# Score products of the recurrent phase in one chain of turns per half, one gate block and the later pins moved

## The chip, the cores and the metric

The kernel runs on one core of a Trainium2 chip. The metric is the device time of one execution in microseconds (us), the median of several runs. The core's engines work beside each other, each through a queue of its own in a fixed order: TensorE (PE, matrix products into PSUM), VectorE (DVE), ScalarE (ACT), GpSimd (POOL), and the queues that issue transfers.

## The reference

One layer of an encoder on `x` of 2048 positions by 1024 features, in float32. It mixes chunked band attention with a recurrent branch (time mixing by a delta rule), and ends with a squared-relu feed-forward. The change touches the recurrent branch:

```python
def step(state, inp):
    r_t, w_t, k_t, v_t, aa_t, bb_t = inp
    sa = jnp.einsum('bhij,bhj->bhi', state, aa_t)
    state = (state * w_t[:, :, None, :] + sa[..., None] * bb_t[:, :, None, :]
             + v_t[..., None] * k_t[:, :, None, :])
    y = jnp.einsum('bhij,bhj->bhi', state, r_t)
    return state, y
...
h = rms_norm(x, pre_mix_g[l])
proj = h @ w_in[l]
...
y_a = chunk_band_attention(q.reshape(shp), k.reshape(shp), v.reshape(shp), rel_bias[l])
y_b = rwkv7_time_mix(p_rwkv, shift_mu[l], w0[l], w2[l], a0[l], a2[l], g2[l],
                     k_k[l], k_a[l], r_k[l], ln_x_w[l], ln_x_b[l])
merged = gate_a * (y_a @ proj_a[l]) + gate_b * (y_b @ proj_b[l])
x = x + rms_norm(merged @ w_out[l], post_mix_g[l])
```

The recurrence runs over all positions for 8 heads of 64. The output of each head is normalised, gets a bonus term and is multiplied by a gate.

## The kernel before

**Groups and phases.** The positions are worked on in 4 groups of 512. Each group passes a recurrent phase (`phase_rwkv`), an attention phase and a merge; after all groups comes the feed-forward. The recurrent phase begins near 25 us of the span in group 0 and repeats every 466 to 496 us.

**The dense matmuls.** The projection by `w_in` is the bulk of TensorE's work there. A block of 128 columns (`dense`) is 24 matmuls of 128x512 in single-pass form: each operand is split into a high and a low part, and 8 each of high by high (`hh,whi`), low by high (`hl,whi`) and high by low (`hh,wlo`) are summed. ACT makes `whi` (L80) and DVE `wlo` (L82). The list `dl` holds the dense matmuls of the phase in their order. A gate block is a `dense` whose result goes through a tanh to memory; nothing in the phase waits for it, so gate blocks fill TensorE while others work.

**The pins.** `place(mm, n)` puts the matmul `mm` behind `dl[n]` in TensorE's queue (`queue_behind`, an order without a semaphore). The tables `BLOCKS`, `TURNED`, `FIFTH`, `BONUS` and `SCORES` hold such numbers. What isn't pinned, and every other engine's order, comes from the program's order and the scheduler that builds the queues.

**The recurrent branch.** The 8 heads are 4 pairs, p = 0 to 3; 512 positions are 8 chunks of 64. Pairs 0 and 1 go through the branch together, then pairs 2 and 3:

1. `rwkv_pre` makes a pair's operands on DVE and ACT, with squared sums (`ps_ss`, L486), bonus (`ps_bonus`, L553) and transposes (`ps_bk`, L564) by TensorE.
2. The **score products** `ps_A` (L584) multiply the operands of 4 chunks at a time (a half), 4 products by the upper 64 rows into one bank of PSUM and 4 by the lower 64 into another. The pool `pa` has two banks, for all that carries the tag "a", the low-rank products `ps_z` and `ps_a` (L427, L428) too. DVE empties each bank by four operations into `NA` (L595, two), `AR` (L601) and `BR` (L602). In the program the two banks take turns product by product; only the first product of pair 0 is pinned.
3. `rwkv_inverse` inverts triangular blocks on DVE: a transpose `N` (L610), 31 steps of `T` and `X` (L620, L626), a transpose `X1` (L629). It runs once for pairs 0 and 1 and once for pairs 2 and 3.
4. `rwkv_blocks` and `rwkv_trans` (`ps_t` L651 and L659, `ps_at` L679, `ps_w`, `ps_ug`, `ps_tq`, `ps_s` L722) make each chunk's transition from it. The first `ps_t` needs `X1`.
5. The chunks follow in order (`rwkv_chunk`): `ps_st` (L737) and `ps_y` (L741) on TensorE, then the state `ST` or `st` on DVE (L742), which the next chunk needs.
6. `rwkv_post` normalises: a square on ACT, a sum `var` on DVE (L755), `var` and a root `grs` on POOL (L756, L758), the product `yn` on DVE (L760), 8 transposes `ps_yt` on TensorE (L769), written out by ACT to `yf` (L774), and the gate `ps_g`.

The steps of pairs 2 and 3 up to their score products run between the steps 4 and 5 of pairs 0 and 1; the steps 6 of pairs 0 and 1 run while the second inverse works.

Of the kernel before, what the change touches and what calls it, by code (L numbers as in the profile page):

```python
# [32 lines left out]

GATES = (0, 0, 1, 0, 0, 0, 0, 1)
STEPS = (1, 2, 1, 1, 1, 1, 1, 1, 1, 1, 1, 0, 0, 2, 1)
BLOCKS = ((412, 424), (631, 644))
TURNED = 438
FIFTH = 494
BONUS = {(0, 1): 138, (1, 0): 258}
SCORES = 150  # L40
DEC = math.exp(-0.5)

ATT0 = 0
# [4 lines left out]
def advance(steps, n=None):  # L48

    while n is None or n > 0:  # L50
        if next(steps, steps) is steps:
            return
        n = n and n - 1


class Block:
# [387 lines left out]
    def rwkv_pre(self, g, p, rp, NA, between=lambda: None):  # L444
        nc = self.nc
# [7 lines left out]
        ps = self.lora(0, p)  # L453
# [5 lines left out]
        ps = self.lora(1, p)  # L459
# [92 lines left out]
        for i, x in enumerate((rh, rl)):  # L552
            mm = nc.tensor.matmul(psb, self.bones, x, start=i == 0, stop=i == 1)  # L553
# [22 lines left out]
        for h in range(2):  # L576
            cs = slice(h * 4, h * 4 + 4)

            both = [self.pa.tile([P, 4, P], F32, tag="a", name="ps_A") for _ in range(2)]
            for j in range(4):  # L580
                c = h * 4 + j
                for par, psA in enumerate(both):
                    rw = slice(par * C, par * C + C)
                    mm = nc.tensor.matmul(  # L584
                        psA[:, j].rearrange("p (s t) -> p s t", t=C),
                        BK[rw, c].rearrange("p s t -> p (s t)"),
                        AR[rw, c, par : 3 : 2 - par], start=True, stop=True,
                    )
                    if p == c == par == 0:
                        self.place(mm, SCORES)  # L590
            for par, psA in enumerate(both):
                ow = slice(C - par * C, P - par * C)
                for lo, w in ((0, C), (32, 32)):
                    hw = slice(par * C + lo, par * C + lo + 32)
                    nc.vector.tensor_tensor(  # L595
                        NA[hw, q, cs, 0:w],
                        psA[hw, :, lo : lo + w],
                        n2[hw, cs, par, None].to_broadcast((32, 4, w)),
                        ALU.mult,
                    )  # L600
                nc.vector.tensor_tensor(AR[ow, cs, par], psA[ow, :, 0:C], mS[ow], ALU.mult)  # L601
                nc.vector.tensor_tensor(BR[:, cs, par, 1], psA[:, :, C:P], mN[:, par, cs], ALU.mult)  # L602
# [38 lines left out]
    def rwkv_blocks(self, NA, Rs, b):  # L641
# [14 lines left out]
        for q in range(2):  # L656
            for c in range(NC):
                for lo, hi in parts:
                    mm = nc.tensor.matmul(ps[lo, q, c], Z[hi, q, c], XT[hi, q, c, 32:64], start=True, stop=True)  # L659
                    second.append(mm)  # L660
        for mm, n in zip((first[0], second[0]), BLOCKS[b]):
            self.place(mm, n)
# [5 lines left out]
    def rwkv_trans(self, p, R):  # L668
# [7 lines left out]
        for h, cs in enumerate(halves):  # L676
            ps = self.pa.tile([P, 4, P], F32, tag="a", name="ps_at")
            for j in range(4):
                mm = nc.tensor.transpose(ps[:, j], AR[:, h * 4 + j, 0:2].rearrange("p s t -> p (s t)"), self.ident)  # L679
                if p == 0 and h == 1 and j == 0:  # L680
                    self.place(mm, TURNED)
            for par in range(2):
# [47 lines left out]
    def rwkv_chunk(self, p, c, R):  # L730
# [5 lines left out]
        for r in rows:  # L736
            mm = nc.tensor.matmul(ps[r], TQ[r, c, 0], S[r], start=True, stop=True)  # L737
            if p == 0 and c == 4 and r.start == 0:
                self.place(mm, FIFTH)
        for r in rows:  # L740
# [6 lines left out]
    def rwkv_post(self, p, R):  # L747
        nc = self.nc
        pc = slice(p * P, (p + 1) * P)
        col = slice(p, p + 1)  # L750
        Y = R["Y"]
        yq = self.tmp("yq").rearrange("p (c t) -> p c t", t=C)
        nc.scalar.activation(yq, Y, AF.Square)
        var = self.sp.tile([P, NC], F32, tag="var", bufs=2, name="var")
        nc.vector.tensor_reduce(var, yq, AX.X, ALU.add)  # L755
        nc.gpsimd.tensor_scalar(var, var, 1.0 / C, GN_EPS, ALU.mult, ALU.add)  # L756
        rs = self.sp.tile([P, NC], F32, tag="grs", bufs=2, name="grs")
        nc.gpsimd.tensor_tensor(rs, var, self.nhalf, ALU.pow)  # L758
        yn = self.tmp("yn").rearrange("p (c t) -> p c t", t=C)
        nc.vector.tensor_tensor(yn, Y, rs[:, :, None].to_broadcast((P, NC, C)), ALU.mult)  # L760
        bv = self.tmp("bv")
        nc.sync.dma_start(bv, self.bvd[p])
        yield
        yf = self.tmp("yf")
        yf3 = yf.rearrange("p (c t) -> p c t", t=C)
        for h in range(2):
            ps = self.pr.tile([C, 4, P], F32, tag="wus", name="ps_yt")
            for j in range(4):
                nc.tensor.transpose(ps[:, j], yn[:, h * 4 + j], self.ident)  # L769
            cs = slice(h * 4, h * 4 + 4)  # L770
            nc.scalar.activation(
                yf3[0:C, cs], ps[:, :, 0:C], AF.Identity, scale=self.gw[0:C, col], bias=self.gb[0:C, col]
            )
            nc.scalar.activation(  # L774
                yf3[C:P, cs], ps[:, :, C:P], AF.Identity, scale=self.gwo[:, col], bias=self.gbo[:, col]
            )
        self.tc.keep_in_program_order(nc.vector.tensor_tensor(yf, yf, bv, ALU.add))
        ps = self.py.tile([P, G], F32, tag="y", name="ps_g")
        self.mm3(ps, [(*(x[:, pc] for x in self.g2), *self.lg)])
        nc.vector.tensor_tensor(yf, yf, ps, ALU.mult)  # L780
        nc.gpsimd.dma_start(self.yd[p], yf)
# [8 lines left out]
    def phase_rwkv(self, g, quads):  # L790
        tc = self.tc
        with ExitStack() as ctx:
# [18 lines left out]
            def gate(n=1):  # L811
                for i in range(n):
                    i = next(gates, None)
                    if i is not None:
                        self.gate(i)
# [12 lines left out]
            def rec_of(NA, Rs, b):  # L828
                self.rwkv_blocks(NA, Rs, b)
                yield  # L830
                for q in range(2):
                    yield from self.rwkv_trans(2 * b + q, Rs[q])
                    yield
                yield from self.recurrence(b, Rs)
# [13 lines left out]
            advance(inv, 6)  # L848
            self.lora_g(g)
            advance(inv)  # L850
            gate()
            rec = rec_of(NA, Rs, 0)
            NA = pairs()
            between = places(STEPS, lambda n: advance(rec, n))
# [15 lines left out]
            for i in range(3):  # L870
# [5 lines left out]
                elif i == 1:  # L876
                    b, c = (rp.tile([P, n, G], F32, tag=t, name="cmb") for t, n in (("AR", 3), ("SV", 2)))
# [763 lines left out]
```

## Time and profile before

| | us |
|---|---|
| median of 3 runs (lowest to highest) | 3209.29 (3207.58 to 3210.35) |
| the profiled execution | 3213.15 |
| its span, first to last instruction | 3211.4 |
| TensorE busy | 3155.3 (98%) |
| VectorE busy | 2236.4 (70%) |
| ScalarE busy | 1577.5 (49%) |
| GpSimd busy | 614.0 (19%) |
| mean granted TensorE clock | 0.998 |

A row of a timeline has the start and the length in us, engine, line, operation, output and inputs, shapes, and a count; in brackets the idle time before it and what ended it. Rows with a count run several instructions together, and pipelined matmuls overlap, so the time that a run of them takes is read from the start of one row to the start of the next. One score product appears as two records of 64 rows, so x16 are the 8 products of a half. A row of waits has the waiting operation, the operation waited for, and us in all, times, and the longest.

### The profile page before, as it was taken

How to read it: one execution, taken by the hardware profiler on the slowest of the kernel's cores; microseconds unless marked ns; L12 is line 12 of the kernel's file. 1: busy time of each engine (PE TensorE's matmuls, PEld its weight loads, DVE VectorE, ACT ScalarE, POOL GpSimd, SP SyncE). 2: the span in 40 equal slices, each digit the busy share in tenths (PEclk: the TensorE clock that was granted, in tenths of full speed). 3: DMA queues.
4: the chain of work that ended last, by engine and by line, in shares of the span. 5: the costliest groups of instructions: out<-in, count | busy, mean ns of one | idle time of the engine just before them, and what ended most of it. 6: DMA issues, size and time to landing. Idle time of an engine off the chain costs nothing. (4 is left out here: it accounts for less than half of the span.)

```text
span 3211.4 us, 49808 instructions
## 1 busy us (share of the span) xinstructions
PE 3155.3 (98%) x18800; PEld 2574.0 (80%) x18800; DVE 2236.4 (70%) x3668; ACT 1577.5 (49%) x2511; POOL 614.0 (19%) x1119
## 2 busy tenths in 40 slices
PE   8999999999999999999999999999999999999998
PEld 6877788777888878888877888888888878888887
DVE  6785667776767786766876775887656668765464
ACT  5435645445745444745534755544543454444343
POOL 3222012132112222112222110122211112210000
PEclk9999999999999999999999999999999999999999
DMA  6245474257574247575336557554887876447565
GB/s 190 85 136 183 134 260 128 60 171 240 178 258 127 78 141 243 178 233 164 96 112 223 168 191 267 191 174 160 290 277 246 282 229 213 164 161 238 195 220 174
DMA packets 436069, 598.82 MB, mean 186 GB/s; under 512 B 25570, under 2 KB 296044, under 8 KB 435828
## 3 DMA queue, kind: packets, MB, share of 16 engines
q1 hardware_dynamic: 377716, 415.24, 41.1%
q0 software_dynamic: 48896, 163.61, 13.8%
q10 hardware_dynamic: 9216, 16.78, 1.4%
q8 instruction: 148, 2.42, 0.3%
q14 instruction: 93, 0.76, 0.1%
HBM read 431.67 MB, written 167.01 MB: 186 GB/s over the span
## 5 line engine op out<-in xcount | busy, mean ns | idle before, releaser
L1465 PE MATMUL ps_dn<-fop 128*128 128x512 f32 x2688 | 610.8, 389 | 0.0
L1465 PEld LDWEIGHTS ps_dn<-fop 128*128 128x128 f32 x2688 | 504.2, 188 | 104.7 <-DVE fop L82 0.3
L80 ACT CAST whi<-wraw 128x1024 fp32r<-128x1024 f32 x232 | 243.4, 1049 | 317.8 <-PE psd L91 235.0
L82 DVE TENSOR_TENSOR wlo<-wraw,whi 128x1024 fp32r<-128x1024 f32 x230 | 280.7, 1220 | 150.0 <-ACT whi L80 96.6
L91 PE MATMUL psd<-hh,whi 128*128 128x512 f32 x1328 | 362.5, 400 | 1.1 <-ACT k L400 1.1
L91 PE MATMUL psd<-hh,wlo 128*128 128x512 f32 x1328 | 356.9, 397 | 0.0
L91 PE MATMUL psd<-hl,whi 128*128 128x512 f32 x1328 | 353.9, 396 | 0.0
L91 PEld LDWEIGHTS psd<-hl,whi 128*128 128x128 f32 x1328 | 244.2, 188 | 48.4
L91 PEld LDWEIGHTS psd<-hh,wlo 128*128 128x128 f32 x1328 | 243.0, 188 | 47.6
L91 PEld LDWEIGHTS psd<-hh,whi 128*128 128x128 f32 x1328 | 240.8, 189 | 49.8 <-ACT k L400 1.6
L82 DVE TENSOR_TENSOR fop<-xraw,fop 128x1024 fp32r<-128x1024 f32 x112 | 137.0, 1223 | 176.5 <-ACT fop L80 176.0
L80 ACT CAST fop<-xraw 128x1024 fp32r<-128x1024 f32 x112 | 117.7, 1051 | 251.2 <-PE ps_dn L1465 188.8
L1335 POOL DMA_DIRECT2D xd<-X x192 | 103.7, 540 | 379.6 <-ACT X L1332 313.3
L82 DVE TENSOR_TENSOR fop<-wdraw,fop 128x1024 fp32r<-128x1024 f32 x112 | 136.6, 1220 | 19.1 <-ACT fop L80 18.6
L80 ACT CAST fop<-wdraw 128x1024 fp32r<-128x1024 f32 x112 | 117.8, 1052 | 36.6 <-DMA wdraw<-in_w_down_dram 20.5
L991 DVE CUSTOM_DVE_ANT_0 sc<-bias,ps_s 128x640 f32<-128x640 f32 (+4 forms) x128 | 93.8, 733 | 48.2 <-PE ps_s L985 24.9
L998 ACT ACTIVATE sc<-sc,mn 128x640 f32<-128x640 f32 (+4 forms) x128 | 97.7, 764 | 27.8 <-DVE mn L991 26.4
L1009 DVE TENSOR_TENSOR PTl<-ps_pt,PTh 128x640 fp32r<-128x640 f32 (+4 forms) x128 | 94.4, 738 | 23.8 <-ACT PTh L1008 22.3
L80 ACT CAST s12h<-s 128x1024 fp32r<-128x1024 f32 x32 | 33.7, 1054 | 156.3 <-PE ps_u L91 155.1
L91 PE MATMUL ps_p<-yh,whi 128*128 128x512 f32 x256 | 101.7, 402 | 2.7 <-ACT yh L80 2.1
L1174 PE MATMUL ps_o<-whi,mh 128*128 128x512 f32 x256 | 100.6, 393 | 2.8 <-DVE o L1185 2.8
L1008 ACT CAST PTh<-ps_pt 128x640 fp32r<-128x640 f32 (+4 forms) x128 | 79.9, 624 | 47.6 <-PE ps_pt L1004 45.8
(374 smaller groups left out, 6854.0 us busy)
## 6 DMA issues: line engine op xcount, KB each, us to landing
wraw<-in_w_in_dram SPq DMA_DIRECT2D x168, 512.0 KB, 4.0
xraw<-xd SPq DMA_DIRECT2D x112, 512.0 KB, 4.5
xd<-X POOLq DMA_DIRECT2D x192, 256.0 KB, 5.1
wraw<-in_w_up_dram SPq DMA_DIRECT2D x80, 512.0 KB, 5.1
wdraw<-wd SPq DMA_DIRECT2D x64, 512.0 KB, 4.8
wdraw<-in_w_down_dram SPq DMA_DIRECT2D x48, 512.0 KB, 5.2
gd<-gate ACTq DMA_DIRECT2D x64, 256.0 KB, 2.4
wd<-cmb POOLq DMA_DIRECT2D x64, 256.0 KB, 3.8
```

The costliest lines, as they stand in the source:

```text
L80: high = self.high = self.nc.scalar.copy(hi, src)
L82: self.low = lower.tensor_tensor(lo, src, hi.bitcast(F32), ALU.subtract).ins
L91: mm.append(nc.tensor.matmul(ps, l, r, start=n == 0, stop=n == last).ins)
L991: least = nc.vector.tensor_tensor_reduce(sc[:, 0:n], bias[:, s0:640], pss[:, c0 : c0 + n], 1.0, 3.0e38, ALU.add, ALU.min, mn,)
L998: nc.scalar.activation(sc[:, 0:n], sc[:, 0:n], AF.Exp, scale=-1.0, bias=mn, accum_out=sm[:, col : col + 1])
L1008: nc.scalar.copy(hv, pst[:, 0:nk])
L1009: nc.vector.tensor_tensor(lv, pst[:, 0:nk], hv.bitcast(F32), ALU.subtract)
L1174: nc.tensor.matmul(ps[t], l[:, k, ts], r[:, k % 2], start=k == 0 and j == 0, stop=k == KB - 1 and j == 2)
L1335: nc.gpsimd.dma_start(self.xd[q][i // 2][:, i % 2], src)
L1465: nc.tensor.matmul(ps, o[:, l, k, sl], o[:, r, k], start=start and n == 0, stop=stop and n == end)
```

## The change

The products of a half form one chain in TensorE's queue, in turns between the two banks. The first product of every half of every pair is pinned by a table `SCORES[p][h]`, where before only that of pair 0 was, and its first number, 150, stays. The transposes `ps_yt` of pair 1 are pinned by a table `TURNS`. A gate block more stands ahead of the first `rwkv_blocks`, so that all gate blocks behind it come one earlier. The pins of `BLOCKS`, `TURNED` and `FIFTH` follow: the first by 24, the length of a block; the second pair of `BLOCKS` by 9.

```diff
--- before.py
+++ after.py
@@ -33,11 +33,12 @@
 
 GATES = (0, 0, 1, 0, 0, 0, 0, 1)
 STEPS = (1, 2, 1, 1, 1, 1, 1, 1, 1, 1, 1, 0, 0, 2, 1)
-BLOCKS = ((412, 424), (631, 644))
-TURNED = 438
-FIFTH = 494
+BLOCKS = ((436, 448), (640, 653))
+TURNED = 462
+FIFTH = 518
 BONUS = {(0, 1): 138, (1, 0): 258}
-SCORES = 150
+SCORES = ((150, 162), (266, 278), (476, 479), (528, 538))
+TURNS = {1: (612, 616)}
 DEC = math.exp(-0.5)
 
 ATT0 = 0
@@ -577,6 +578,7 @@
             cs = slice(h * 4, h * 4 + 4)
 
             both = [self.pa.tile([P, 4, P], F32, tag="a", name="ps_A") for _ in range(2)]
+            last = None
             for j in range(4):
                 c = h * 4 + j
                 for par, psA in enumerate(both):
@@ -586,8 +588,11 @@
                         BK[rw, c].rearrange("p s t -> p (s t)"),
                         AR[rw, c, par : 3 : 2 - par], start=True, stop=True,
                     )
-                    if p == c == par == 0:
-                        self.place(mm, SCORES)
+                    if last is None:
+                        self.place(mm, SCORES[p][h])
+                    else:
+                        self.queue_behind(mm.ins, last)
+                    last = mm.ins
             for par, psA in enumerate(both):
                 ow = slice(C - par * C, P - par * C)
                 for lo, w in ((0, C), (32, 32)):
@@ -766,7 +771,9 @@
         for h in range(2):
             ps = self.pr.tile([C, 4, P], F32, tag="wus", name="ps_yt")
             for j in range(4):
-                nc.tensor.transpose(ps[:, j], yn[:, h * 4 + j], self.ident)
+                mm = nc.tensor.transpose(ps[:, j], yn[:, h * 4 + j], self.ident)
+                if j == 0 and p in TURNS:
+                    self.place(mm, TURNS[p][h])
             cs = slice(h * 4, h * 4 + 4)
             nc.scalar.activation(
                 yf3[0:C, cs], ps[:, :, 0:C], AF.Identity, scale=self.gw[0:C, col], bias=self.gb[0:C, col]
@@ -848,7 +855,7 @@
             advance(inv, 6)
             self.lora_g(g)
             advance(inv)
-            gate()
+            gate(2)
             rec = rec_of(NA, Rs, 0)
             NA = pairs()
             between = places(STEPS, lambda n: advance(rec, n))
```

Lines below the new tables shift by one, and by two to five behind the new statements (L584 is L586, L737 is L742, L769 is L774). Three places in the queues show what moves.

TensorE from the end of pair 1's transition (`ps_s`) to the first chunks of pairs 0 and 1, between which pair 2's score products and the low-rank products of pair 3 stand. Before:

```order
L722 MATMUL ps_s_1742<-SV,BR 64x64 x16
L584 MATMUL ps_A<-AR,BK 128x128 x8
L91 MATMUL psd<-hh,wlo 128x512 x4
L584 MATMUL ps_A<-AR,BK 128x128 x4
L91 MATMUL psd<-hh,wlo 128x512 x2
L584 MATMUL ps_A<-AR,BK 128x128 x4
L737 MATMUL ps_st<-st_101,TQ 64x64 x2
L741 MATMUL ps_y<-st_101,TQ 64x64 x2
L737 MATMUL ps_st<-st_102,TQ 64x64 x2
L741 MATMUL ps_y<-st_102,TQ 64x64
L427 MATMUL ps_z<-lora,whw 128x512
L428 MATMUL ps_z<-lora,wlw 128x512
```

and of the change:

```order
L727 MATMUL ps_s_1776<-SV,BR 64x64 x16
L92 MATMUL psd<-hh,wlo 128x512 x3
L586 MATMUL ps_A<-AR,BK 128x128 x8
L92 MATMUL psd<-hh,wlo 128x512 x3
L742 MATMUL ps_st<-st_101,TQ 64x64 x2
L746 MATMUL ps_y<-st_101,TQ 64x64 x2
L742 MATMUL ps_st<-st_102,TQ 64x64 x2
L746 MATMUL ps_y<-st_102,TQ 64x64 x2
L586 MATMUL ps_A<-AR,BK 128x128 x8
L742 MATMUL ps_st<-ST,TQ 64x64 x2
L746 MATMUL ps_y<-ST,TQ 64x64 x2
L742 MATMUL ps_st<-ST,TQ 64x64 x2
```

The first half has moved behind 3 dense matmuls and the second behind one chunk of both pairs, each in one row of 8; the second, in two rows of 4 before with 2 dense between, has 3 dense and a chunk ahead of it instead of 4 dense; `ps_z` and `ps_a`, the next behind the second piece's end, now follow two whole chunks.

VectorE behind the first half of pair 3's score products, where the last states of pairs 0 and 1 (`st`), the sums and products of `rwkv_post` and the start of the second inverse (`N`) meet. Before:

```order
L601 TENSOR_TENSOR AR<-ps_A,mS 64x4x64
L602 TENSOR_TENSOR BR<-ps_A,mN 128x4x64
L742 SCALAR_TENSOR_TENSOR st_101<-ps_st,gC,S_1577 128x64
L742 SCALAR_TENSOR_TENSOR st_102<-ps_st,gC,S_1741 128x64
L755 TENSOR_REDUCE var<-yq 128x8
L610 STREAM_TRANSPOSE N<-NA 128x1024
L760 TENSOR_TENSOR yn<-ps_y,grs 128x512
L755 TENSOR_REDUCE var<-yq 128x8
L620 TENSOR_TENSOR T<-N,X 128x31
L82 TENSOR_TENSOR wlo<-wraw,whi 128x1024
L760 TENSOR_TENSOR yn<-ps_y,grs 128x512
```

and of the change:

```order
L760 TENSOR_REDUCE var<-yq 128x8
L765 TENSOR_TENSOR yn<-ps_y,grs 128x512
L600 TENSOR_TENSOR NA<-ps_A,n_2027 32x256
L600 TENSOR_TENSOR NA<-ps_A,n_2027 32x4x32
L606 TENSOR_TENSOR AR<-ps_A,mS 64x4x64
L607 TENSOR_TENSOR BR<-ps_A,mN 128x4x64
L600 TENSOR_TENSOR NA<-ps_A,n_2027 32x256
L600 TENSOR_TENSOR NA<-ps_A,n_2027 32x4x32
L606 TENSOR_TENSOR AR<-ps_A,mS 64x4x64
L607 TENSOR_TENSOR BR<-ps_A,mN 128x4x64
L760 TENSOR_REDUCE var<-yq 128x8
L615 STREAM_TRANSPOSE N<-NA 128x1024
```

The first `yn` stood behind the evacuations of the second half and behind `N`; it now stands ahead of these evacuations, directly behind its `var`, and `N` stands behind both.

TensorE from pair 1's output transposes to the first `ps_t` of the second inverse. Before:

```order
L91 MATMUL psd<-hh,whi 128x512
L769 MATMUL ps_yt<-ident,yn 64x128 x4
L91 MATMUL psd<-hh,whi 128x512 x2
L769 MATMUL ps_yt<-ident,yn 64x128 x4
L91 MATMUL psd<-hh,whi 128x512 x5
L91 MATMUL psd<-hl,whi 128x512 x8
L91 MATMUL psd<-hh,wlo 128x512 x8
L91 MATMUL psd<-hh,whi 128x512 x8
L91 MATMUL psd<-hl,whi 128x512 x8
L91 MATMUL psd<-hh,wlo 128x512 x8
L91 MATMUL psd<-hh,whi 128x512 x8
L651 MATMUL ps_t_2512<-X_2414,NA 32x32 x32
```

and of the change:

```order
L92 MATMUL ps_g<-lora_g,g2l 128x512
L92 MATMUL psd<-hh,whi 128x512 x8
L92 MATMUL psd<-hl,whi 128x512 x5
L774 MATMUL ps_yt<-ident,yn 64x128 x4
L92 MATMUL psd<-hl,whi 128x512 x3
L92 MATMUL psd<-hh,wlo 128x512
L774 MATMUL ps_yt<-ident,yn 64x128 x4
L92 MATMUL psd<-hh,wlo 128x512 x7
L92 MATMUL psd<-hh,whi 128x512 x8
L92 MATMUL psd<-hl,whi 128x512 x8
L92 MATMUL psd<-hh,wlo 128x512
L656 MATMUL ps_t_2546<-X_2448,NA 32x32 x32
```

The two rows of 4 transposes stand behind 13 and another 4 dense matmuls, where they stood behind 1 and 2. The `ps_t` stands behind 24 dense matmuls from the last transposes on where 53 stood before, and behind 102 from the last score product of pair 3 on where 123 stood.

At the end of the phase, the transposes of pair 2 stand behind 16 dense matmuls after the last chunk, where they stood behind 31. In pair 1, each half's products are one row of 8 with 12 dense between the halves, where four rows of 4 stood with 2 dense between.

## Prediction

> **What bounds the kernel now.** I read the page's busy table first, then the waits of TensorE (PE) grouped by line, and then the timelines of PE, VectorE (DVE) and GpSimd (POOL) through the recurrent phase of group 0. Times there are us from the start of the span.
>
> ```profile
> span 3211.4 us, 49808 instructions
> PE 3155.3 (98%) x18800; PEld 2574.0 (80%) x18800; DVE 2236.4 (70%) x3668; ACT 1577.5 (49%) x2511; POOL 614.0 (19%) x1119
> ...
> PE ps_yt L769 <- ACT yf L774: 7.2, 4, 2.0
> PE ps_st L737 <- DVE ST L742: 4.2, 4, 1.1
> PE ps_g L91 <- DVE yn L760: 1.5, 4, 0.4
> ```
>
> PE is busy for 98% of the span, so time can leave only as work of PE (with the price of changing between kinds of matmul) or as a wait of PE, some 56 us in all. The waits that the change can touch are few: 7.2 us for the output transposes, 4.2 for the fifth chunk, 1.5 for the gating product. Whatever the change adds to PE's waits counts in full, four times, once for each group of 512 positions. The dense matmuls, 128x512, fill PE between everything else; their number does not change, so a term is what remains when they are counted out.
>
> ```profile
> 55.92 1.75 PE L91 MATMUL psd<-hh,whi 128*128 128x512 f32 x7
> 57.60 1.16 PE L584 MATMUL ps_A<-AR,BK 64*128 64x128 f32 x16
> 58.69 0.50 PE L91 MATMUL psd<-hh,whi 128*128 128x512 f32 x1
> 59.03 1.55 PE L91 MATMUL psd<-hl,whi 128*128 128x512 f32 x6
> 60.55 1.13 PE L584 MATMUL ps_A<-AR,BK 64*128 64x128 f32 x8
> 61.60 0.73 PE L91 MATMUL psd<-hl,whi 128*128 128x512 f32 x2
> 62.27 1.16 PE L584 MATMUL ps_A<-AR,BK 64*128 64x128 f32 x8
> 63.35 2.12 PE L91 MATMUL psd<-hh,wlo 128*128 128x512 f32 x8
> 65.31 0.39 PE L427 MATMUL ps_z<-lora,whw 128*128 128x512 f32 x1
> ```
>
> This stretch holds both forms of the score products. A dense matmul costs 0.227 from start to start (8 of them, 1.81, in the long runs). The first half of pair 0 runs as turns between two banks: 55.92 to 59.03 is 3.11, less 8 dense 1.82, leaves **1.29**; the products themselves are 58.69 less 57.60, 1.09, so one change to small products and back costs 0.20. The second half is split into one bank after the other: 59.03 to 65.31 is 6.28, less 16 dense 3.63, leaves **2.65**.
>
> **The packing.** Five halves of each group are split before and become turns: the second of pair 0, both of pair 1, the second of pairs 2 and 3. Each saves 2.65 less 1.29, 1.36. The rest of this part is what holds those gains back.
>
> ```profile
> 58.79 0.71 DVE L595 TENSOR_TENSOR NA<-ps_A,n 32x256 f32<-32x256 f32 x2 [1.39 <-PE ps_A L584]
> ...
> 60.43 0.73 DVE L595 TENSOR_TENSOR NA<-ps_A,n 32x256 f32<-32x256 f32 x2
> 61.18 0.42 DVE L601 TENSOR_TENSOR AR<-ps_A,mS 64x256 f32<-64x256 f32 x1
> 61.52 0.41 DVE L602 TENSOR_TENSOR BR<-ps_A,mN 128x256 f32<-128x256 f32 x1
> ```
>
> DVE begins 1.19 after the first product of a half (57.60 to 58.79), frees the first bank 2.8 after it and the second at 61.93, **4.33 after it**. Where the next half comes sooner, its second product waits, and a chain lets none behind it pass. Pairs 0 and 1 have about 12 dense between halves: 1.29 and 2.72 make 4.0, so 0.3 of waiting each. Net for pairs 0 and 1: three times 1.36 less 0.6, a gain of **3.5** a group.
>
> A rule speaks against the edit: the Trainium skill, page "TensorEngine Tiling (Array Packing)", section on performance considerations, says that tiling speeds up TensorE but not PSUM evacuation; the rows above agree. By it these waits and those of pair 2 stand; without it the sum below would be some 9 us lower, four times 0.6 and 1.7.
>
> **Pair 2** has the gap that is too short.
>
> ```profile
> 165.62 2.02 PE L584 MATMUL ps_A<-AR,BK 64*128 64x128 f32 x16
> 167.56 1.20 PE L91 MATMUL psd<-hh,wlo 128*128 128x512 f32 x4
> ...
> 172.13 0.50 PE L427 MATMUL ps_z<-lora,whw 128*128 128x512 f32 x1
> ...
> 173.27 0.48 PE L427 MATMUL ps_a<-lora,wha 128*128 128x512 f32 x1
> ...
> 174.86 2.11 PE L91 MATMUL psd<-hh,whi 128*128 128x512 f32 x8 [0.27 <-ACT k L400]
> ```
>
> Before, 165.62 to 174.86 is 9.24 with 6 dense. From here on I set the times of after against those of before at the end of ps_s, 165.62: the dense moved ahead of the first inverse shift both engines alike, and the first half starts at 166.5, 3 dense and a change later. After, only 3 dense and one chunk stand between the halves: the second is reached 2.6 after the first's first product and blocked until 4.4, a wait of 1.7. Its banks then hold the two low-rank products behind it, which use the same pool: ps_z until its first bank is free (7.3 after the start, a wait of 1.3) and ps_a until the second is (8.8, a wait of 0.9); with the third chunk, which now stands here, the dense are reached after 10.0. Against 9.24 less 3 dense 0.68 plus that chunk's 0.6 and a change of 0.2 this is **1.1 a group lost**: the waits of 3.9 eat the packing (1.36 and the first half's 1.94 less 1.09) and the small waits that go. Its ends: a gain of 2.0 if DVE kept up, a loss of 1.5 without the waits that go.
>
> The squared sums of pair 3 follow 1.3 later than before, DVE waits for them, and the fifth chunk with its old wait of 1.06 now waits about **0.3** longer, since PE has lost less than DVE there.
>
> **Pair 3 and the second inverse** are the largest term.
>
> ```profile
> 193.82 1.49 PE L584 MATMUL ps_A<-AR,BK 64*128 64x128 f32 x16
> ...
> 195.13 0.71 DVE L595 TENSOR_TENSOR NA<-ps_A,n 32x256 f32<-32x256 f32 x2 [0.75 <-PE ps_A L584]
> ...
> 201.96 0.67 DVE L755 TENSOR_REDUCE var<-yq 128x8 f32<-128x512 f32 x1
> 202.55 2.04 DVE L610 STREAM_TRANSPOSE N<-NA 128x1024 f32<-128x1024 f32 x1
> ...
> 209.07 0.69 DVE L760 TENSOR_TENSOR yn<-ps_y,grs 128x512 f32<-128x512 f32 x1 [1.82 <-POOL grs L758]
> ...
> 231.60 1.19 DVE L629 STREAM_TRANSPOSE X<-X 128x512 f32<-128x512 f32 x1
> ...
> 202.72 0.20 POOL L756 TENSOR_SCALAR var<-var 128x8 f32<-128x8 f32 x1 [0.56 <-DVE var L755]
> 203.00 1.67 POOL L758 TENSOR_TENSOR grs<-var,nhalf 128x8 f32<-128x8 f32 x1
> 206.08 1.22 POOL L756 TENSOR_SCALAR var<-var 128x8 f32<-128x8 f32 x1 [1.41 <-DVE var L755]
> ```
>
> The packing here gains 1.36 and 0.33 (the first half's 1.41 against 1.09), less a bank wait of 0.25 and a further change of 0.20: **1.2 a group**. But DVE falls behind. With 0.9 from the start of pair 2, 0.8 from its waits and more dense ahead of them, the first half's products start near 196.0 and, with DVE at 1.2 behind and 3.1 long, their evacuation ends at 200.3, the states and the first var at 201.3. Next in DVE's queue now stands the first yn, which waits for POOL: var and root take 0.20 and 1.67 and some hand-over, 2.1 here, up to 3.1 if POOL's var takes the 1.22 of the third row. Behind that waiting yn stand the eight evacuations of the second half, though their products end at 201.55. They run from 204.0 to 207.1; the transpose that starts the inverse begins at 207.6 instead of 202.55, 5.0 later. Behind it one split, one var and one yn with its 1.82 of waiting no longer lie: 30.2 (202.55 to 232.8) less 4.1 is 26.1, so the inverse is ready at **233.7**.
>
> ```profile
> 220.07 0.63 PE L769 MATMUL ps_yt<-ident,yn 128*64 128x128 f32 x4 [2.02 <-ACT yf L774]
> ...
> 221.66 2.48 PE L91 MATMUL psd<-hh,whi 128*128 128x512 f32 x5
> 223.94 2.49 PE L91 MATMUL psd<-hl,whi 128*128 128x512 f32 x8
> 226.27 1.98 PE L91 MATMUL psd<-hh,wlo 128*128 128x512 f32 x8
> ...
> 235.43 0.76 PE L651 MATMUL ps_t<-X,NA 32*32 32x32 f32 x36
> ...
> 221.50:225.00 3.50, 3.50 (x12) 2.81 (x10) 3.12 (x12) 1.94 (x4) 0.54 (x1) 0.51 0.86 242
> ```
>
> PE comes there sooner: 102 dense instead of 123 lie between the last score product and ps_t. Before, 200.03 to 235.43 is 35.4; less 123 dense 27.9, the wait 2.0 and the slow stretch of 1.5 (below), 4.0 remain for the small products. After: 201.55 plus 23.2 plus 4.0 is 228.7 at most, 228.3 with its small gaps gone. So PE waits **5.4 a group** where it waited for nothing. If DVE lost none of its new idle time (2.1 for POOL, 1.3 for the sums and 0.6 at the banks) the inverse would be ready at 229.7 and the wait 1.4; if POOL were slow, 6.4. I take 5.4, since the POOL rows stand for the very operations.
>
> **The transposes.** Pinned 13 dense later (2.95) the second pair's no longer waits 2.02 and the other's 4 dense cover the little it had: 7.2 over the row, **1.8 a group gained**. Ends: nothing to 2.1.
>
> **The clock.** After that wait of 2.0 the granted clock was 0.51 in the last row, a window's (its last three numbers are clock, DMA share and GB/s): 5 dense took 2.28 for 1.14 and 8 took 2.33 for 1.81, 1.5 lost beyond the 0.1 of a change. It happened in group 0 alone. That drop goes with its wait, but one of 5.4 us is far longer, so I count 1.5 in every group: **4.5 more in all**. Ends: 1.5 less than before (none) to 9 (two windows each in three groups). The Trainium skill, page "TensorE: Matmul & The Clock Gate", part on the HAM clock gate, gives a free-running window of 3.4 us; an idle one puts PE at half clock. By the page alone a wait of 5.4 holds no whole window for sure, and the drops could be fewer: the first rival's time. This case's drop came after only 2.0 us of idling.
>
> **The end of the phase.** The gate block moved ahead leaves 16 dense instead of 31 before the transposes of pair 2: 15 times 0.227 is 3.4 less cover for the root, yn and DVE's var, which already ran out by the 0.4 of the ps_g row. How much was left at the first transposes no row shows: the ends are 0 and 3.8, and I take **2.4** a group, nearer to the upper, for ps_g stood at the edge already. Ahead of the first inverse the same block only adds cover; no line of the waits names ps_t there.
>
> **The sum.** A group: -3.5 (pairs 0 and 1), +1.1 (pair 2), +0.3 (fifth chunk), -1.2 (pair 3), -1.8 (transposes), +5.4 (inverse), +2.4 (end): +2.7. Four groups: +10.8; the clock +4.5; together +15.3. The profiled execution took 3213.15 (span 3211.4 and 1.75 around it), so 3228.5. It was 3.9 above the median of 3209.29, so **3224.6**; attention's smaller waits may give back a little, and I say **3224**.
>
> **The rivals.** *Waits without the clock*, the drop as rare as before or gone: +10.8 less up to 1.5, 3218 to 3220. For it: the three other waits at ps_yt, 1.7 each by their sum, dropped nothing. Against it: the new wait is longer than those by 3. Chance 0.2.
> *DVE stays ahead, faster than before*: the wait at the second inverse does not occur. Place: the yn ahead of the evacuations of pair 3. Its price is the 5.4 a group, 21.6 in all, and the drops; it decides whether X is ready by 228.3. Then the group is at -2.7, so -10.8 and -1.5: 3197; at the bound of 229.7, +1.4 a group, 3203. For it: DVE is busy for 70% only. Against it: 26.1 of the inverse are back to back, and the start is late by waits that queue order fixes. Chance 0.2.
> *The change doesn't cost what I say anywhere*: all packing kept (3.5+2.0+1.2) and 1.8 of the transposes, nothing lost: 8.5 a group and 1.5, 3174. Against it stands 4.33 for emptying two banks. Chance 0.05.
> *Worse*: POOL's slow var, two windows of clock: 3233 to 3240. Chance 0.05.
>
> **How the numbers follow.** Forecast 0.5, 3220 to 3233. 0.2% is 6.4 us, about what a measurement of this kernel can tell from no change: faster is below 3202.9, slower above 3215.7. Faster: 0.05 and 0.13 of the second rival, 0.18. Within: its other 0.07 and 0.15 from small errors of the first rival and the forecast, 0.22. Slower: 0.60. The range, 3197 to 3233, leaves out the packing kept whole and the worst.
>
> **What would show it.** Right: ps_t of the second inverse waits 4 to 6.5 on DVE in each group, with a clock near half behind it; ps_A of pair 2 waits 1.7 on DVE; no wait for yf at ps_yt; the transposes of the phase's end wait for yn; PE's busy time, apart from slow windows, falls by some 25 us. Wrong: the inverse's X ends before PE arrives, or DVE's yn ahead of the evacuations waits for nothing.

## The result, and the profile after

| | us |
|---|---|
| before, median | 3209.64 |
| after, median of 4 runs (lowest to highest) | 3257.62 (3256.93 to 3260.33) |
| ratio, with its 95% interval | 1.0143 (1.0131 to 1.0155) |
| predicted | 3224 (3197 to 3233) |

The change makes the kernel slower, as forecast, but by 48 us and not by 15. The busy table of the changed kernel's page:

```profile
span 3258.6 us, 49835 instructions
...
PE 3156.7 (97%) x18800; PEld 2572.4 (79%) x18800; DVE 2235.3 (69%) x3668; ACT 1578.1 (48%) x2511; POOL 627.8 (19%) x1119
```

And the waits of its TensorE that grew or are new (waiting operation, operation waited for, us in all, times, longest):

```profile
PE ps_t L656 <- DVE X L634: 21.3, 4, 5.3
...
PE ps_st L742 <- DVE ST L747: 6.6, 4, 1.6
PE ps_yt L774 <- DVE yn L765: 6.4, 4, 1.6
PE ps_g L92 <- DVE yn L765: 5.5, 4, 1.4
PE ps_A L586 <- DVE BR L607: 5.4, 8, 1.1
PE ps_s L992 <- DMA KK<-kc: 4.8, 2, 2.4
PE ps_pt L1011 <- DVE VV L962: 4.2, 3, 1.4
...
PE ps_z L428 <- DVE BR L607: 2.7, 4, 1.0
PE ps_s L992 <- ACT KK L948: 2.6, 1, 2.6
...
PE psd L92 <- DVE QA L941: 1.9, 2, 1.6
...
PE ps_s L992 <- DVE KK L949: 1.4, 1, 1.4
PE ps_a L428 <- DVE BR L607: 1.3, 4, 0.3
```

PE's idle time grew from 56.1 to 101.9 us (span less busy), 45.8. The list says where: 21.3 for the second inverse, 9.4 for the banks of pair 2, 2.4 more for the fifth chunk, about 10 more for yn at the end of the phase, and 14.9 at the start of attention, in five rows that the list of before doesn't have. Against them the 7.2 for yf are gone, and smaller waits and other idle time give back some 5. The surprise is the first number of PE's row on the page. The packing should have taken some 30 us out of PE's busy time, and it rose by 1.4. Either the packing did nothing, or PE ran slower. The windows view over all stretches in which the granted clock was 0.50 settles which (stretch, its length, busy time of PE, PEld, DVE, ACT and POOL, then clock, DMA share, GB/s):

```profile
174.22:181.05 6.83, 5.53 (x31) 3.58 (x26) 5.93 (x16) 4.48 (x8) 1.16 (x2) 0.50 0.00 0
194.70:198.12 3.42, 3.42 (x12) 2.32 (x13) 1.75 (x5) 0.42 (x1) 0.00 (x0) 0.50 0.53 147
235.66:245.90 10.24, 7.35 (x77) 5.92 (x77) 7.31 (x15) 3.07 (x5) 3.14 (x5) 0.50 0.46 144
307.34:310.75 3.41, 3.27 (x8) 2.63 (x9) 2.04 (x4) 0.73 (x3) 0.70 (x1) 0.50 0.39 129
652.09:658.91 6.82, 6.12 (x45) 4.09 (x42) 5.66 (x14) 3.60 (x6) 0.43 (x1) 0.50 0.00 0
713.53:720.36 6.83, 5.03 (x72) 4.29 (x73) 4.53 (x9) 2.39 (x4) 3.13 (x5) 0.50 0.42 119
...
sum 78.52, PE 67.34 PEld 51.35 DVE 57.92 ACT 33.75 POOL 20.82; mean PE 5.18 PEld 3.95 DVE 4.46 ACT 2.60 POOL 1.60
```

There are 13 such stretches ahead of the span's last microseconds, 78.5 us, with 67.3 us of PE work in them; at half clock half of it is lost, 33.7. Before had one, 3.4 us long, 1.7 lost. So the ledger of the span is: idle +45.8, clock +32.0, and work of PE without the clock -30.6 (3156.7 less 33.7, against 3155.3 less 1.7), together +47.2, the difference of the spans. The split between the last two terms is an estimate: dense matmuls take twice as long in such a stretch (next rows), small ones somewhat less (the 64 ps_t below take 1.85 from start to start, and 1.13 at full clock in the run with the filler), so 32.0 is an upper end, and whatever comes off it comes off the 30.6 too. It is not far off: in the changed kernel and the four runs below that keep its score products, PE's busy time less half of what falls into these stretches, and less the filler, is 3122 to 3127.

A timeline of the changed kernel's PE at the second inverse shows a wait and the clock behind it in one place:

```profile
232.82 0.39 PE L92 MATMUL psd<-hh,wlo 128*128 128x512 f32 x1
238.55 1.92 PE L656 MATMUL ps_t<-X,NA 32*32 32x32 f32 x64 [5.34 <-DVE X L634]
240.40 3.35 PE L92 MATMUL psd<-hh,wlo 128*128 128x512 f32 x7
243.56 2.63 PE L92 MATMUL psd<-hh,whi 128*128 128x512 f32 x6
```

The wait is 5.34. Behind it 7 dense matmuls take 3.16 (240.40 to 243.56) in place of 1.59. VectorE ahead of it, in the same kernel:

```profile
205.66 0.67 DVE L760 TENSOR_REDUCE var<-yq 128x8 f32<-128x512 f32 x1
208.42 0.69 DVE L765 TENSOR_TENSOR yn<-ps_y,grs 128x512 f32<-128x512 f32 x1 [2.08 <-POOL grs L763]
209.02 0.70 DVE L600 TENSOR_TENSOR NA<-ps_A,n 32x256 f32<-32x256 f32 x2
```

The yn waits 2.08 for POOL with the evacuations of pair 3's second half queued behind it.

### The profile page after: what moved, and what is told of

It reads as the page before. It is cut to its first block, busy times and chain, and to the rows that moved or that the text cites. A ratio compares the mean times of both kernels' runs of the same rounds, so it can differ in the third digit from the quotient of the medians.

```text
span 3258.6 us, 49835 instructions
## 1 busy us (share of the span) xinstructions
PE 3156.7 (97%) x18800; PEld 2572.4 (79%) x18800; DVE 2235.3 (69%) x3668; ACT 1578.1 (48%) x2511; POOL 627.8 (19%) x1119
## 5 line engine op out<-in xcount | busy, mean ns | idle before, releaser
L92 PE MATMUL psd<-hl,whi 128*128 128x512 f32 x1328 | 361.8, 397 | 0.0
L92 PEld LDWEIGHTS psd<-hh,whi 128*128 128x128 f32 x1328 | 249.3, 194 | 53.0 <-issue 1.7
L81 ACT CAST s12h<-s 128x1024 fp32r<-128x1024 f32 x32 | 33.7, 1054 | 154.8 <-PE ps_u L92 153.8
L92 PE MATMUL ps_p<-yl,whi 128*128 128x512 f32 x256 | 102.8, 402 | 0.3 <-DVE yl L83 0.2
```

Source lines behind the costliest of these rows:

```text
L81: high = self.high = self.nc.scalar.copy(hi, src)
L92: mm.append(nc.tensor.matmul(ps, l, r, start=n == 0, stop=n == last).ins)
```

## The experiments

Times are given as the difference to the median of before on the same chip, since medians of before vary between 3209.6 and 3213.5 from chip to chip. "Half clock" is the total length of the stretches at clock 0.50 in the profiled execution, without the last microseconds of the span.

| run | over before, us | ratio (95% interval) | half clock, us |
|---|---|---|---|
| the change | +48.0 | 1.0143 (1.0131 to 1.0155) | 78.5 |
| filler in the wait for the inverse | +38.3 | 1.0119 (1.0104 to 1.0134) | 54.6 |
| pair 2 as before | +33.5 | 1.0106 (1.0091 to 1.0121) | 54.6 |
| yn behind the evacuations | +42.3 | 1.0134 (1.0118 to 1.0149) | 81.9 |
| ps_t 27 dense later | +23.5 | 1.0075 (1.0060 to 1.0090) | 54.6 |
| pair 2 as before and ps_t later | +11.2 | 1.0036 (1.0022 to 1.0049) | 17.1 |
| gate block alone, on before | +27.6 | 1.0083 (1.0066 to 1.0100) | 23.9 |
| pairs 0 and 1 alone, on before | +32.5 | 1.0099 (1.0084 to 1.0115) | 61.4 |
| attention's first products later | +47.9 | 1.0149 (1.0135 to 1.0163) | 61.4 |
| transposes alone, on before | -3.6 | 0.9989 (0.9979 to 0.9999) | 0 |
| the same, ps_t 6 dense later | -4.3 | 0.9985 (0.9976 to 0.9994) | 0 |
| the same, with pair 0 | -7.5 | 0.9974 (0.9964 to 0.9984) | 0 |

**A filler in the wait.** Useless matmuls keep PE busy while it waits for the inverse; nothing else changes.

```diff
         ps = self.pa.tile([P, 2, NC, 32], F32, tag="a", name="ps_t1")
+        if b == 1:
+            wide = ps.rearrange("p q c t -> p (q c t)")
+            idle = [nc.tensor.matmul(wide, self.h[0][:, 0, 0:P], self.h[0][:, 0], start=True, stop=True) for _ in range(22)]
+            for mm in idle:
+                self.place(mm, BLOCKS[b][0])
```

> The changed kernel with 22 useless matmuls of 128x512 into the bank of the second inverse's first ps_t, ahead of it in TensorE's queue and overwritten by it. They take 5.0 us, about the 5.3 that TensorE waits there, so ps_t starts when it did. The clock theory: no idle window, so the slow windows behind that wait (from 235, 713, 1222 and 1731 us, 23.2 us of busy time, 11.6 lost) go: 3244 to 3248. The rival (the clock follows the small products of ps_t and behind it, or costs little because what follows waits anyway): no change within 3 us of 3257.6.

```profile
233.52 5.15 PE L655 MATMUL ps_t<-hh 128*128 128x512 f32 x22
239.09 1.20 PE L661 MATMUL ps_t<-X,NA 32*32 32x32 f32 x64 [0.42 <-DVE X L634]
240.22 1.90 PE L92 MATMUL psd<-hh,wlo 128*128 128x512 f32 x7
241.96 1.54 PE L92 MATMUL psd<-hh,whi 128*128 128x512 f32 x6
```

In this timeline of the run's PE the 22 matmuls stand in the wait, ps_t starts no sooner, and the 7 dense behind it take 1.74. No half-clock stretch follows the wait in any group, though PE does 5 us of work more each time, and 9.7 us come off where 10 to 14 were expected (the two intervals just overlap). So this wait costs twice: its length, and the clock behind it. Not all of the clock comes back: the total falls by 24 us of half clock, not by the 30.7 of those four stretches, since others begin or last longer elsewhere.

**Pair 2 as before.** Its products are neither pinned nor chained.

```diff
                 for par, psA in enumerate(both):
...
+                    if p == 2:
+                        continue
                     if last is None:
                         self.place(mm, SCORES[p][h])
```

> The changed kernel, but the score products of pair 2 are neither pinned nor chained, as before the change. The clock theory (the new waits leave windows of 3.41 us in which TensorE does too little, and the halved clock behind them is what costs): the waits of pair 2 at ps_A, ps_z and ps_a (2.65 a group) go, with them the slow windows that begin at 174, 652, 1157 and 1669 us (27.5 us of busy time at half clock, 13.8 lost) and perhaps those at 195 and 1690 (3.4 lost); 2.2 a group of packing are given back. In all 15 to 20 us less than the changed kernel: 3238 to 3243. The rival (the slow windows come with the small products themselves, and waits alone count): 2.65 less 2.2 a group, 1 to 3 us less: 3255 to 3257, with the slow windows still there.

The windows view of this run over pair 2 and over the wait behind it:

```profile
171.00:178.00 7.00, 6.58 (x59) 4.75 (x58) 6.01 (x17) 3.09 (x5) 0.00 (x0) 1.00 0.00 1
232.00:242.00 10.00, 7.80 (x141) 6.48 (x141) 6.72 (x12) 3.08 (x5) 3.27 (x6) 0.66 0.49 157
```

The clock stays at 1.00 in pair 2, in all four groups, and falls behind the second inverse as in the change. 14.5 us come off, just under the clock theory's 15 to 20 and far from the rival's 1 to 3. Pair 2's waits are short, none over 1.07 us and 9.4 in all, about what the packing given back is worth (2.2 a group); most of the 14.5 is the clock behind them.

**The yn behind the evacuations**, on VectorE's queue:

```diff
-                nc.vector.tensor_tensor(BR[:, cs, par, 1], psA[:, :, C:P], mN[:, par, cs], ALU.mult)
+                done = nc.vector.tensor_tensor(BR[:, cs, par, 1], psA[:, :, C:P], mN[:, par, cs], ALU.mult)
+                self.last_score = done.ins
...
-        nc.vector.tensor_tensor(yn, Y, rs[:, :, None].to_broadcast((P, NC, C)), ALU.mult)
+        mm = nc.vector.tensor_tensor(yn, Y, rs[:, :, None].to_broadcast((P, NC, C)), ALU.mult)
+        if p == 0:
+            self.queue_behind(mm.ins, self.last_score)
```

> The changed kernel with one order on VectorE: the yn of pair 0 stands behind the evacuations of pair 3's second half, as before the change. Prediction's step (the waiting yn holds the evacuations up by 2.4): the second inverse is ready some 2 to 2.5 earlier, the wait at ps_t falls from 5.3 to 3 a group, and 8 to 10 us come off, 1 to 3 more by the shorter slow windows: 3245 to 3250. If the start of the inverse is set by something else: no change, 3258.

The row of the waits for the inverse in this run:

```profile
PE ps_t L657 <- DVE X L635: 13.0, 4, 3.5
```

It was 21.3: the mechanism is right, 8.3 of waiting go. The time falls by only 5.7, and the intervals overlap, so that a gain in time is not shown. A shorter wait did not give less half clock (81.9 against 78.5).

**ps_t 27 dense later**, so that it stands where the inverse is ready:

```diff
-BLOCKS = ((436, 448), (640, 653))
+BLOCKS = ((436, 448), (667, 680))
```

> The changed kernel with the second pair of BLOCKS 27 dense matmuls later (667, 680), so that ps_t stands where the inverse is ready. The clock theory: the wait of 5.3 a group goes (21.3) and the slow windows behind it (11.6), 33 us together; but 27 dense fewer (6.1 us) are left as cover behind the phase, of which some comes back as waits at the start of attention, where about 10 us in all are new already. 3225 to 3240. If the wait alone counted: 21 less the new waits, 3240 to 3250.

24.5 us come off, at the good end of the range. The wait for X is gone from the list, and so are the stretches behind it but for one. Part comes back where the cover is now short: 4.8 us at ps_y and 2.9 at ps_s of the transition. Attention doesn't get worse, against what was expected: of the 14.9 at its first products 8.1 are left, all at the keys.

**Both repairs at once**, pair 2 as before and ps_t later:

> The changed kernel with both repairs: pair 2 as before, and the second pair of BLOCKS 27 dense later. If the two losses are apart from each other: 14.5 and 24.5 less than the changed kernel's 48 over before, so 9 above before, 3221 with before at 3212. What is left over before is then the end of the phase and attention. If they share their loss (DVE is late once, for both): 3232 to 3235.

11.2 over before: the two losses add. The clock is the smaller part of what is left (17.1 us, at most half of it, 8.6, lost); waits in the transition of pairs 2 and 3 (ps_y), at the end of the phase and in attention stand in the list of this run:

```profile
PE ps_y L733 <- ACT SV L708: 7.2, 3, 4.1
PE ps_g L92 <- DVE yn L767: 6.3, 4, 1.6
PE ps_yt L776 <- DVE yn L767: 6.1, 4, 1.5
PE ps_s L994 <- DMA KK<-kc: 5.2, 2, 3.5
```

**The gate block alone.** The kernel before, with the block ahead of the first ps_t and every later pin 24 later:

```diff
-BLOCKS = ((412, 424), (631, 644))
-TURNED = 438
-FIFTH = 494
+BLOCKS = ((436, 448), (655, 668))
+TURNED = 462
+FIFTH = 518
...
-            gate()
+            gate(2)
             rec = rec_of(NA, Rs, 0)
```

> The kernel before with one part of the change alone: the gate block moved ahead of the first ps_t, and all later pins 24 dense matmuls later; score products and transposes as before. The cover theory: what is late at the end of the phase and at the start of attention in the changed kernel (6.4 us for yn at ps_yt, 4 more at ps_g, some 14 at the first products of attention, each with slow windows behind it, 5 to 7 lost) comes from this block alone: 25 to 32 us above before, 3237 to 3244 on a chip with before at 3212. The rival (those waits come from pairs 2 and 3 and the second inverse being late): at most 12 above before, 3224 at most.

```profile
PE ps_yt L769 <- ACT yf L774: 8.0, 4, 2.5
PE ps_yt L769 <- DVE yn L760: 6.5, 4, 1.6
PE ps_s L985 <- DMA KK<-kc: 5.8, 2, 3.0
PE ps_g L91 <- DVE yn L760: 5.4, 4, 1.4
...
PE ps_pt L1004 <- DVE VV L955: 4.2, 3, 1.4
PE ps_s L985 <- ACT whi L80: 3.6, 1, 3.6
```

27.6 over before, in the range of the cover theory. The waits for yn (6.5 and 5.4) and for VV are those of the changed kernel to within a tenth, with the score products untouched, and attention's first products wait 16.6 in all against 14.9. So the end of the phase and attention are late because 24 dense matmuls that covered them now stand ahead of the first inverse. The profiled execution took 3247.6, 9.1 above the median of its four, so these waits and the half clock may be at the upper end for this kernel.

**Attention's first products later.** In the changed kernel's queue the first two ps_s of attention stand ahead of a whole dense block, in the one before behind it; this run puts them back.

```diff
-                            nc.tensor.matmul(
+                            mm = nc.tensor.matmul(
...
+                            if p == par + qb + lo_ + i == 0:
+                                self.queue_behind(mm.ins, self.mm[-1])
```

> The changed kernel with one order in attention: its first two products ps_s stand behind the third block of dense, as before the change, not ahead of its 24 matmuls. If this order is what attention lost (12 us of waits at KK and QA, slow windows from 307, 782 and 1290, 4.9 us lost): 10 to 15 less than the changed kernel, 33 to 38 above before. If the end of the phase is simply late (fewer dense as cover): the waits move to the next products, and 0 to 4 come off.

The first theory is refuted: the time is the same. The waits of this run show where they went:

```profile
PE psd L92 <- DVE QA L941: 13.9, 4, 3.5
```

The waits for the keys are gone, and the dense block that now stands first waits 3.5 in every group for VectorE to empty its bank. The order of the queue decides only which matmul waits; the lateness is that of VectorE behind the end of the phase.

**Pairs 0 and 1 alone**, on the kernel before:

```diff
-SCORES = 150
+SCORES = ((150, 162), (266, 278))
...
-                    if p == c == par == 0:
-                        self.place(mm, SCORES)
+                    if p < 2:
+                        if last is None:
+                            self.place(mm, SCORES[p][h])
+                        else:
+                            self.queue_behind(mm.ins, last)
+                        last = mm.ins
```

> The kernel before with the chains of pairs 0 and 1 alone, at their new pins; the gate block isn't moved. The packing theory: 3.1 a group comes off these pairs, 12 us in all, but TensorE's queue has ps_t 24 dense later and no dense between the halves of pair 2, so the banks are waited for there (3.2 a group, and up to 2 at ps_z and ps_a) with slow windows behind (3 a group): 12 less, 20 to 30 more, 3220 to 3232. If the packing stays (no slow windows, DVE in time): 3200.

At +32.5, 3243.4, it lies beyond what was expected, 3220 to 3232, and the loss isn't where it was expected: the waits for the banks of pair 2 are 7 us in all (2.4 at ps_A, the rest at ps_z and ps_a) where up to 21 were, 8.2 are at a dense block behind ACT, 4.4 at the inverse, and the half clock, 61.4 us, costs some 29 where 12 were expected. The scheduler put ps_t 24 dense later by itself, and squeezed what lies between it and pair 2. So the packing of these two pairs did not pay in this order of the queue. That the missing dense there is the reason is likely but not tried by itself; the block that the change moves there is missing later.

**The parts that gain.** The transposes of pair 1 alone, on the kernel before:

```diff
+TURNS = {1: (588, 592)}
...
+                if j == 0 and p in TURNS:
+                    self.place(mm, TURNS[p][h])
```

> The kernel before with one part of the change alone: the transposes ps_yt of pair 1 pinned 12 and 14 dense matmuls later, as the change does counted from the same dense. Both theories: the waits for yf go (7.2 us) and with them the one slow window of group 0 (1.5): 8 to 9 less than before, 3200 to 3202. If the wait only moves to another place: 3208 to 3210.

3.6 come off and not 8 to 9. The waits for yf are gone, and so is the half-clock stretch of group 0, but this run's list has new ones:

```profile
PE ps_t L652 <- DVE X L630: 4.7, 4, 1.3
...
PE ps_s L723 <- DVE TQ L716: 2.3, 3, 1.7
```

Without its old wait PE reaches the inverse before it is ready: of the 8.7 (7.2 of waiting and 1.5 of clock) 7.0 reappear in these two rows. The next run puts ps_t 6 dense later (`BLOCKS = ((412, 424), (637, 650))`):

> The kernel before with the transposes of pair 1 pinned 12 and 14 dense later, as in the run with these alone, and the second pair of BLOCKS 6 dense later (637, 650), where that run waited 1.2 a group for the inverse. If that wait was what became of the rest of the gain: 4 to 5 us less than that run's ratio of 0.9989, a ratio near 0.9975. If the gain only moves on to the next wait (ps_s behind TQ, or the end of the phase): 0.9985 to 1.0.

The wait for X goes, and the ratio, 0.9985, can't be told from the 0.9989 before: 4.1 stand at ps_s and 2.5 at ps_at instead. The second of the two expectations holds. The last adds the second half of pair 0 as one chain of turns (`SCORES = (150, 162)`, for p = 0 alone):

> The kernel of the run before it in this list, and the second half of pair 0 as one chain of turns behind dense 162, as in the change. TensorE saves 1.36 a group less a bank wait of 0.3, 4.2 us in all; where the first inverse is reached 1.1 sooner, up to all of it comes back as a wait, unless pair 1's products and so the inverse come sooner as well. The packing theory: 3 to 4 us less than the run before it. The other: no change.

3.1 less than the run before it by medians, as the packing theory has it, but the intervals overlap. Against the kernel before, 0.9974 (0.9964 to 0.9984) is a gain, with busy time of PE at 3149.7 and not one half-clock stretch ahead of the span's end. It has the lowest ratio of all these kernels, though that of the run before it can't be told from it.

## Why the prediction went wrong

**Right: the sign, and most steps.** The packing took some 30.6 us of work off PE by the ledger; the terms of the prediction make 30.3 (four times five halves of 1.36, 0.85 and 0.33, less two changes of 0.20), though it named only "some 25" as the sign of being right. The second inverse: 5.4 predicted, 5.34 measured, by the step that was named, a yn that waits 2.1 for POOL (2.08) with the evacuations behind it; taking it out brought 8.3 of waiting back. The transposes no longer wait for yf. The end of the phase: 2.4 predicted; 1.6 at ps_yt and 1.4 less 0.4 at ps_g are 2.6. The fifth chunk: 0.3 more predicted, 0.6 measured. Counted from the end of ps_s, TensorE and the inverse both arrive over 3 us later than forecast, behind two half-clock stretches, and the difference of the two holds.

The bank waits elsewhere, 0.3 in pairs 0 and 1 and 0.25 in pair 3, are in no row of the waits, but they stand inside PE's busy time. Pair 1's two halves in group 0 of the changed kernel:

```profile
91.04 1.16 PE L586 MATMUL ps_A<-AR,BK 64*128 64x128 f32 x16
92.13 1.42 PE L92 MATMUL psd<-hh,whi 128*128 128x512 f32 x5
...
95.09 1.54 PE L586 MATMUL ps_A<-AR,BK 64*128 64x128 f32 x16
96.56 0.50 PE L92 MATMUL psd<-hl,whi 128*128 128x512 f32 x1
```

From start to start the first half takes 1.09 and the second 1.47, 0.38 more; in pair 3 the second takes 1.31 to 1.33, 0.24 more.

The sign was in good part luck all the same. Without the clock's 32.0 and attention's 14.9, below, the ledger comes to 0.3 (a few us more if the clock cost less), where the prediction had 10.8 for all but the clock.

**Too high:** the waits of pair 2, 3.9 predicted, 2.35 a group measured by the three rows (5.4, 2.7 and 1.3 over four), of which ps_A has 1.35 and not 1.7. Three sums around them don't come out as written, though none moves the forecast by as much as 1 us: pair 2's loss is 1.0 by its own terms and not 1.1, without the waits that go it is 1.9 (2.0 less 3.9) and not 1.5, and the "9 us lower" counts one of pair 2's three waits.

**The step that failed is the clock.** The prediction counted "1.5 in every group: 4.5 more in all", with 9 as the upper end. Measured, the clock took 33.7 against 1.7: 32 us. Of the 33 by which the sum of 15 fell short, this term has 27.5. Three things in it were wrong. Only the longest wait was priced, while the waits of pair 2, 1.07 and 0.96 the longest, set off half clock in all four groups; taking them away brought 14.5 us. A half-clock stretch was taken to be over after 3.4 us and 1.5 of loss, while those behind ps_t last 6.8 to 10.2, and PE's work in the first of them was 7.35, 3.7 lost. And the three old waits that had dropped nothing (1.7 on average) were weighed against new waits by length alone; they stood among dense matmuls, while those of pair 2 stand among small products, and the windows of the last section speak for a difference between the two.

**The term that was missing is attention.** That "attention's smaller waits may give back a little" had the wrong sign: 14.9 us of new waits at its first products. The prediction followed the moved gate block to the end of the phase, where it was right, and not one step further, to what the missing dense had covered there. The gate block alone, on the kernel before, costs 27.6. The other terms, pair 2's waits above all (6.2 less than forecast), take part of these two back.

**The rivals.** That the clock would be as rare as before is refuted by the 13 stretches, that VectorE would stay ahead by 21.3 us of waiting, that the packing would be kept whole by the ratio. The one called *Worse*, at 0.05, named two windows of clock, the right direction, and still ended some 18 us short at 3240; its other half, a slow var on POOL, did not occur (yn waited 2.08).

## What to carry to other kernels

Where TensorE is busy for 98%, its work is not the only price: before moving matmuls about, count for each stretch how much of every few microseconds is idle or filled with small products, since a wait may halve the clock for a stretch longer than itself. Filler that is moved ahead of one wait is missing at another; follow it to the next phase, and take it only where nothing behind it needs it. A gain of TensorE alone, ahead of a chain on another engine, reappears as a wait for that chain, as the two runs with the transposes alone showed.

## What was not expected of the hardware

All half-clock stretches of a trace begin on one grid of 3.413 us (174.22 and 1730.70 lie 456 steps apart), whatever stands there. Cutting the ten traces that have such a stretch into these windows (the last 40 us or so of the span left out), by PE's busy share in the window ahead, with bounds that were chosen from these traces:

| busy share of a window at full clock | next at full clock | next at half clock |
|---|---|---|
| under 0.45 | 0 | 55 |
| 0.45 to 0.65 | 103 | 36 |
| over 0.65 | 8938 | 1 |

The Trainium skill, page "TensorE: Matmul & The Clock Gate", part on the HAM clock gate, has the free-running window of 3.4 us, and these traces agree. It asks for an idle window before the clock halves; here a window less than 0.45 busy was always enough, and one of 0.60 was at times.

In the range between, what PE is busy with goes along with the outcome. Of its 139 windows, 77 hold hardly any small products (under 1% of the window; matmuls that are neither 128x512 nor transposes), and none of these was followed by half clock. In 53 the small products take 12% or more, and 35 of these were; of the 9 others, 1 was. Small products therefore seem to count for less than dense matmuls, by this comparison of windows; no run changed that alone.

Half clock also ends by the grid: of the half-clock windows in these traces that were less than 0.8 busy, 28 of 28 were followed by another at half clock, while of those at 0.95 or more 84 of 91 were followed by full clock. So a stretch lasts until one of its windows is nearly full, which took two or three behind the second inverse.
